# A two-block kernel whose first mixer begins with half of the features: modulation, tokens and weight rows come in two halves of the model width

## The chip, the cores and the metric

The kernel runs on one core of one Trainium2 chip. The metric is the device time of one execution, in microseconds (us). The engines are TensorE (PE; its weight loads are shown as PEld), VectorE (DVE), ScalarE (ACT), GpSimd (POOL) and SyncE (SP), whose queue issues nearly all DMA transfers.

## The reference: what is computed

Two transformer blocks, one after the other, on 256 tokens of width 1024 in float32. The change touches only the beginning of the first block:

```
mod = (jax.nn.silu(c) @ w_ada[l] + b_ada[l])[:, None, :]
shift_m, scale_m, gate_m, shift_f, scale_f, gate_f = jnp.split(mod, N_MOD, axis=-1)
h = rms_norm(x, g_mix[l]) * (1.0 + scale_m) + shift_m
x = x + gate_m * hybrid_mixer(h, w_in[l], b_forget[l], g_out_a[l], g_out_b[l], w_out[l])
...
proj = h @ w_in
(aq, ak, av, iq, ik, iw, bq, bk, bv, bf) = jnp.split(
    proj, list(np.cumsum(IN_SPLITS)[:-1]), axis=-1)
```

So the mixer's input `h` needs two of the six modulation vectors, `scale_m` (piece 1 of `w_ada`) and `shift_m` (piece 0), each a product of a vector of 1024 with a 1024 x 1024 part of `w_ada` (4 MB). Then come ten projections of `h` by column groups of `w_in` (1024 x 2896). After the mixer follow a mixture of 32 experts and the second block, which no line of the change touches.

## The kernel before, in words

All matrices are streamed from device memory once, in pieces of 1 MB (8 KB on each of 128 partitions), into a ring of 11 buffers (`raw`); an issue waits on SP until its buffer has been read for the last time. The SP queue issues in program order: four pieces of `w_ada` piece 0, `x`, four pieces of `w_ada` piece 1, and then the columns of `w_in` by projection (`iq`, `ik`, `bq`, `bk`, ...). Behind each load up to two small loads are let out of a list (`trickle`).

`ada(v)` makes modulation vector `v`. A piece of `w_ada` brings 2 of the 8 rows that each partition holds (row 8p+j lies on partition p), and 4 matmuls per piece (tile `p_ada`) sum them over all 8; the trace shows 8 rows for these 4. ScalarE copies the sums out (`part`), small matmuls turn them into columns (`p_col`), and VectorE adds the bias (`modcol`). The two square sums of `x`, `rstd`, and the normed tokens `xn` (shown as `prob`, whose buffer they use) follow from `x`; TensorE turns `xn` in 16 transposes (`p_tr`). `ac` is (1 + scale) times `g_mix`. `scaled` then makes the 8 slices (`j` = 0 to 7, 128 features each) of the turned and modulated input: `hTh` on ScalarE (rounded to fp32r), `full` on VectorE, and the rest `hTl` on VectorE or GpSimd.

Each projection is a generator of four steps of two slices `j` each. A step first cuts its weights in a high and a low part (`wih` on ScalarE, line 86; `wil` on VectorE, line 87) and then runs 24 matmuls (`p_w`: 2 slices, 4 column blocks, 3 products hi-hi, hi-lo, lo-hi). A projection's sums stay in two PSUM banks over its four steps. A string of letters sets the order of these steps: `i` (iq), `q` (bq), `k` (ik, iw and bf together), `b`, `v`, `a`, `n` are steps of projections, capitals are steps of the attention, of the indexer and of the rest; `F` begins with the matmul `p_dup`, which needs the result of `k`. The weights of a step are cut one step ahead of its products: where a letter is met, the products of the step before it are issued. Each engine's instructions run in the order in which they were issued or in which the framework's scheduler placed them; `held` fixes the order of those that it marks while `holding` is set.

In the kernel before, all 8 slices are modulated first, and then the string begins with `iiqikqqF`, so that the products ahead of `p_dup` are seven steps: i0, i1, i2, q0, i3, k, q1.

Of the kernel before, what the change touches and what calls it, by code (L numbers as in the profile page):

```python
# [7 lines left out]
FT = mybir.dt.float32  # L8
# [3 lines left out]
AF = mybir.ActivationFunctionType  # L12
OP = mybir.AluOpType
# [3 lines left out]
T = 256  # L17
D = 1024
# [14 lines left out]
def tile_block(ctx: ExitStack, tc: tile.TileContext, A, out):  # L33
# [12 lines left out]
    def bank(shape, name):  # L46
        return ps.tile(shape, FT, name=name, tag="bank")
# [5 lines left out]
    def load(name, shape, *src):  # L53
        n = 1
        for s in shape:
            n *= s
        t = raw.tile([128, RAW], FT, name=name, tag="raw")
        v = t[:, :n]
        if len(shape) == 2:
            v = v.rearrange("p (a b) -> p a b", a=shape[0])  # L60
        for i, s_ in enumerate(src):
            n = shape[0] // len(src)
            tc.keep_in_program_order(nc.sync.dma_start(v[:, n * i:n * i + n] if len(src) > 1 else v, s_))
        for _ in range(2):
            if trickle:
                dst, src_ = trickle.pop(0)
                tc.keep_in_program_order(nc.sync.dma_start(dst, src_))
        return v

    def load_cols(name, dname, width, c0, n, j0, nj):  # L70
        return load(name, (nj, n), dram(dname, j0 * width + c0,
                                        [[8 * width, 128], [width, nj], [1, n]]))

    holding = []

    def held(ins):
# [22 lines left out]
    def mm(o, lhsT, rhs, start, stop):  # L99
        held_pe(pe.matmul(o, lhsT, rhs, start=start, stop=stop, skip_group_check=True))  # L100
# [15 lines left out]
    c8 = const.tile([128, 8], FT, name="c8")  # L116
    act.dma_start(c8, dram("c", 0, [[8, 128], [1, 8]]))
    bcol = const.tile([128, 6, 8], FT, name="bcol")
    act.dma_start(bcol, dram("b_ada", 0, [[8, 128], [D, 6], [1, 8]]))
    gcol = const.tile([128, 2, 8], FT, name="gcol")  # L120
    act.dma_start(gcol[:, 0], dram("g_mix", 0, [[8, 128], [1, 8]]))
# [11 lines left out]
    def win_load(c0, n):  # L133
        return [load_cols(f"win{c0}_{k}", "w_in", WIN, c0, n, 4 * k, 4) for k in range(2)]

    xt = const.tile([128, 2, D], FT, name="xt")
    modrow = const.tile([128, 2, D], FT, name="modrow")
# [15 lines left out]
    aqk = raw2.tile([128, 8, T], FT, name="aqk", tag="raw2")  # L153
    aqT, akv, ikw, ikT = aqk[:, 0:4], aqk[:, 4:6], aqk[0:80, 6], aqk[:, 7]
    prob1 = raw2.tile([128, 8, T], FT, name="prob1", tag="raw2")
    for _ in range(4):
        ada_piece(0)
    tc.keep_in_program_order(nc.sync.dma_start(xt, dram("x", 0, [[D, 128], [128 * D, 2], [1, D]])))
    for _ in range(4):
        ada_piece(1)  # L160
    def small_load(dst, src):
        trickle.append((dst, src))

    w_bf = const.tile([128, 8, 8], FT, name="w_bf")
# [163 lines left out]
    def ada(v):  # L328
# [28 lines left out]
            dve.tensor_tensor(modcol[:, v - v // 3], p, bcol[:, v], op=OP.add)  # L357
        yield

    def gate_row():  # L360

        m = modrow[:, 1]
        for q in range(4):
            for jj in range(2):
                w = wada[5][q][:, jj]
                act.activation(w, w, AF.Copy, scale=cs[:, 2 * q + jj:2 * q + jj + 1])
                pool.tensor_tensor(m, m, w, op=OP.add)
            yield
# [26 lines left out]
        act.activation(junk, src, AF.Square, accum_out=s)  # L395
        return s

    def transpose_block(src, banks, t):
        for j in range(8):
            pe.transpose(banks[j // 2][:, j % 2, t * 128:t * 128 + 128], src[:, j::8], ident)  # L400

    def transposes(src, by_column=False):

        out_ = [bank([128, 2, T], "p_tr") for _ in range(4)]
        if by_column:
            for j in range(8):
                for t in range(2):
                    pe.transpose(out_[j // 2][:, j % 2, t * 128:t * 128 + 128], src[:, t, j::8], ident)
        else:
            for t in range(2):  # L410
                transpose_block(src[:, t], out_, t)
        return out_

    def scaled(banks, scale, bias, hi, lo, keep):

        for j in range(8):
            p = banks[j // 2][:, j % 2]
            sc = scale[:, j:j + 1]
            if bias is None:
                act.activation(hi[:, j], p, AF.Copy, scale=sc)  # L420
                dve.scalar_tensor_tensor(lo[:, j], p, sc, f32(hi[:, j]), op0=OP.mult, op1=OP.subtract)
            else:
                act.activation(hi[:, j], p, AF.Identity, bias=bias[:, j:j + 1], scale=sc)
                full = keep.tile([128, T], FT, name="full", tag="fin", bufs=3)
                dve.tensor_scalar(full, p, sc, bias[:, j:j + 1], op0=OP.mult, op1=OP.add)
                (dve if j % 2 else pool).tensor_tensor(lo[:, j], full, f32(hi[:, j]), op=OP.subtract)
# [8 lines left out]
    next(g1)  # L438
    xTb = [bank([128, 2, T], "p_tr") for _ in range(4)]
    for t in range(2):  # L440
        transpose_block(xn[:, t], xTb, t)
        next(g1)
    for _ in g1:
        pass
# [408 lines left out]
    def router_weights():  # L853
        dve.scalar_tensor_tensor(af, modcol[:, 3], 1.0, gcol[:, 1], op0=OP.add, op1=OP.mult)

        p = bank([36, 1], "p_rb")
        for j in range(8):
            mm(p, wr[:, j], bf_[:, j:j + 1], j == 0, j == 7)
        dve.tensor_tensor(wr, wr, af[:, :, None].to_broadcast([128, 8, 36]), op=OP.mult)
        dve.tensor_tensor(rb, rb, p, op=OP.add)  # L860
        rbr = const.tile([128, 36], FT, name="rbr")
        rbb = a1.tile([36, 128], FT, name="rbb", tag="fin", bufs=3)
        dve.tensor_copy(rbb, rb.to_broadcast([36, 128]))
        p = bank([128, 36], "p_rb")
        mm(p, rbb, ident[:36, :36], True, True)
        dve.tensor_copy(rbr, p)
        const_["rbr"] = rbr
        yield
# [8 lines left out]
            "Z": router_weights()}  # L877
    p_ = None
    for c in "iiqikqqFqXFXbbYYbbvY5TXXF22XY25XY5v5vYXYXv2BWBa2aaBYBnGB3BC33CCCC3BCanB3C!CR4D4D4D4E4DDDEoEHoEoDEoDEEESZpppp":
        if c == "!":  # L880
            flush()
        elif c == "p":
            if p_ is None:
                p_ = proj_out(1, *oa, rsa)
            main([next(p_)], 0)
        elif c.islower():
            main([next(work[c])], 0)
        else:
            next(work[c])
# [1060 lines left out]
```

## Time and profile before

| | before |
|---|---|
| runs (median, lowest to highest) | 741.2 us (740.72 to 742.93, 3 runs) |
| the profiled execution | 738.99 us, its span 737.2 us |
| mean granted TensorE clock | 0.966 |
| busy over the span: PE, DVE, ACT, POOL | 660.9, 402.3, 311.4, 88.9 us |
| moved by DMA | 196.94 MB, mean 267 GB/s |

The span runs from the first to the last instruction; the device time lies 1.79 us above it. A granted clock of 1.00 is TensorE's upper level (2.4 GHz), 0.50 its lower one (1.2 GHz). Matmul ends are modelled, so that a TensorE shown as busy isn't at its peak.

### The profile page before, as it was taken

To read this page: it belongs to the slowest core of one execution; us is meant where nothing else is said; L and a number is where in the kernel's file an instruction comes from. 1 tells how busy PE (TensorE), PEld (TensorE's weight loads), DVE (VectorE), ACT (ScalarE), POOL (GpSimd) and SP (SyncE) were. 2 spreads that over 40 slices of the span, in tenths; PEclk is the share of its full clock that TensorE was granted. 3 is DMA by queue.
4 is the path that set the end of the run, shared out by engine and by line. 5 is a ranking of instruction groups with operands and counts; after the bars stand their busy time and mean duration, and the time that the engine had idled before them with its cause. 6 is when DMAs were issued, how large, how long until landed. Compare 5 with 4: busy or idle time off the path is not lost. (4 is left out here: it accounts for less than half of the span.)

```text
span 737.2 us, 13263 instructions
## 1 busy us (share of the span) xinstructions
PE 660.9 (90%) x5489; PEld 510.4 (69%) x5489; DVE 402.3 (55%) x737; ACT 311.4 (42%) x513; POOL 88.9 (12%) x87
## 2 busy tenths in 40 slices
PE   5799996999899775998876989999999999999996
PEld 1498774877765333444442489987899999898994
DVE  2367978575663230423312269959676555555555
ACT  1446556564741010201110177685455444444445
POOL 7010309910000000000000063010000000000001
PEclk9899998999989998999988999999999999999999
DMA  9999779995639899998999999653445555550001
GB/s 342 372 382 359 257 273 292 307 405 206 261 133 421 322 421 415 405 397 332 422 418 420 374 370 387 212 172 116 138 149 172 172 192 201 177 199 34 1 1 57
DMA packets 69203, 196.94 MB, mean 267 GB/s; under 512 B 7550, under 2 KB 33219, under 8 KB 57350
## 3 DMA queue, kind: packets, MB, share of 16 engines
q1 hardware_dynamic: 67558, 195.30, 70.5%
q8 instruction: 53, 0.87, 0.5%
q10 hardware_dynamic: 1216, 0.30, 0.2%
q0 software_dynamic: 352, 0.28, 0.1%
q14 instruction: 24, 0.20, 0.1%
HBM read 194.81 MB, written 1.05 MB: 266 GB/s over the span
## 5 line engine op out<-in xcount | busy, mean ns | idle before, releaser
L100 PE MATMUL p_gu<-Xl,wguh 128*128 128x256 f32 x352 | 99.8, 284 | 0.0
L100 PE MATMUL p_gu<-Xh,wgul 128*128 128x256 f32 x352 | 99.3, 283 | 0.0
L100 PE MATMUL p_gu<-Xh,wguh 128*128 128x256 f32 x352 | 98.9, 283 | 0.1
L100 PEld LDWEIGHTS p_gu<-Xl,wguh 128*128 128x128 f32 x352 | 67.5, 192 | 0.5
L100 PEld LDWEIGHTS p_gu<-Xh,wguh 128*128 128x128 f32 x352 | 67.1, 192 | 0.7 <-ACT Xh L1379 0.4
L100 PEld LDWEIGHTS p_gu<-Xh,wgul 128*128 128x128 f32 x352 | 67.4, 192 | 0.3 <-DVE wgul L87 0.2
L100 PE MATMUL p_gu<-eg,xg 128*32 128x256 f32 x576 | 41.8, 416 | 15.3 <-PEq L1296 9.5
L87 DVE TENSOR_TENSOR wdnl<-wdn,wdnh 128x1024 fp32r<-128x1024 f32 x22 | 27.0, 1225 | 32.4 <-ACT wdnh L86 32.4
L100 PEld LDWEIGHTS p_gu<-eg,xg 128*32 128x32 f32 x576 | 19.7, 118 | 36.0 <-issue 24.4
L1149 DVE TENSOR_TENSOR sl<-sl,p_gu 128x256 f32<-128x256 f32 x9 | 3.8, 422 | 69.2 <-ACT sl L1148 69.2
L1148 ACT ACTIVATE sl<-p_gu 128x256 f32<-128x256 f32 x9 | 3.5, 384 | 87.9 <-PE p_gu L100 87.9
L100 PE MATMUL p_w<-hTh,wih 128*128 128x256 f32 x128 | 37.7, 297 | 2.5 <-ACT wih L86 2.5
L100 PE MATMUL p_dn<-ed,aT 128*32 128x512 f32 (+2 forms) x304 | 34.5, 573 | 5.2 <-ACT aT L1156 5.0
L86 ACT ACTIVATE wdnh<-wdn 128x1024 fp32r<-128x1024 f32 x22 | 23.3, 1058 | 36.5 <-PE p_gu L100 35.9
L87 DVE TENSOR_TENSOR wgul<-wup,wguh 128x1024 fp32r<-128x1024 f32 x22 | 27.0, 1226 | 21.3 <-ACT wguh L86 20.2
L1066 ACT ACTIVATE xg<-p_xg,modcol,af 128x128 f32<-128x128 f32 x36 | 15.6, 462 | 53.2 <-DVE xg L1068 53.0
L87 DVE TENSOR_TENSOR wgul<-wgt,wguh 128x1024 fp32r<-128x1024 f32 x22 | 27.0, 1225 | 19.8 <-ACT wguh L86 19.8
L86 ACT ACTIVATE wguh<-wgt 128x1024 fp32r<-128x1024 f32 x22 | 23.3, 1061 | 33.7 <-PE p_gu L100 18.2
L100 PE MATMUL p_w<-Xh,w2h 128*128 128x256 f32 x128 | 37.0, 289 | 0.5 <-ACT w2h L86 0.4
L100 PE MATMUL p_w<-Xh,w2l 128*128 128x256 f32 x128 | 36.3, 285 | 1.1 <-DVE w2l L87 0.6
L100 PE MATMUL p_w<-hTl,wih 128*128 128x256 f32 x128 | 36.9, 289 | 0.0
L100 PE MATMUL p_gu<-eu,xg 128*32 128x256 f32 x576 | 35.2, 379 | 1.9 <-DMA eu<-in_w_up_dram 1.9
(625 smaller groups left out, 1645.0 us busy)
## 6 DMA issues: line engine op xcount, KB each, us to landing
eg<-in_w_gate_dram SPq DMA_DIRECT2D x32, 1024.0 KB
eu<-in_w_up_dram SPq DMA_DIRECT2D x32, 1024.0 KB
ed<-in_w_down_dram SPq DMA_DIRECT2D x28, 1024.0 KB
wada<-in_w_ada_dram SPq DMA_DIRECT2D x24, 1024.0 KB
w<-in_w_in_dram SPq DMA_DIRECT2D x11, 1024.0 KB
wgt<-in_w_gate_up_dram SPq DMA_DIRECT2D x11, 1024.0 KB
wup<-in_w_gate_up_dram SPq DMA_DIRECT2D x11, 1024.0 KB
wdn<-in_w_down_dram SPq DMA_DIRECT2D x11, 1024.0 KB
```

What stands on the lines that cost most here:

```text
L86: held(act.activation(hi, src, AF.Copy))
L87: held(eng.tensor_tensor(lo, src, f32(hi), op=OP.subtract))
L100: held_pe(pe.matmul(o, lhsT, rhs, start=start, stop=stop, skip_group_check=True))
L1066: act.activation(xg[:, j], b[:, jj], AF.Identity, bias=bf_[:, j:j + 1], scale=af[:, j:j + 1])
L1148: act.activation(st.s[:st.n], st.b[:st.n, 0:256], AF.Silu)
L1149: dve.tensor_tensor(st.s[:st.n], st.s[:st.n], st.b[:st.n, 256:512], op=OP.mult)
```

## The change

Feature rows are dealt out anew for the first mixer: slices 0 to 3 now hold features 0 to 511 (four to a partition), slices 4 to 7 features 512 to 1023. `ada_cols(v, h)` makes one half (512 columns) of one modulation vector from two loads of 1 MB. `turn_half(h)` transposes one half of the tokens, and `modulated(h)` joins the two. The first half is made ahead of all products, the second is a letter of its own, `1`, in the string. The first halves of `w_in` for `iq` and `bq` are loaded ahead of the second halves of `w_ada`, and the string begins with `iqq1iikqF`, so that the products ahead of `p_dup` are i0, i1, q0, then q1, then i2, i3, k: the same seven steps.

```diff
+    def load_cols(name, c0, n, k=None):
+        src = [dram("w_in", 512 * WIN * h + c0, [[4 * WIN, 128], [WIN, 4], [1, n]]) for h in range(2)]
+        return load(name, (8, n), *src) if k is None else load(name, (4, n), src[k])
...
-    act.dma_start(bcol, dram("b_ada", 0, [[8, 128], [D, 6], [1, 8]]))
+    act.dma_start(bcol[:, 3:5], dram("b_ada", 3 * D, [[8, 128], [D, 2], [1, 8]]))
+    for v in range(2):
+        act.dma_start(bcol[:, v].rearrange("p (h j) -> p h j", h=2),
+                      dram("b_ada", v * D, [[4, 128], [512, 2], [1, 4]]))
...
+    def ada_half(v, h):
+        wada[v, h] = [load(f"wada{v}_{h}_{q}", (4, 512), dram("w_ada", 4 * q * 6 * D + v * D + 512 * h,
+                                                              [[8 * 6 * D, 128], [6 * D, 4], [1, 512]]))
+                      for q in range(2)]
...
-    for _ in range(4):
-        ada_piece(0)
+    ada_half(1, 0)
     tc.keep_in_program_order(nc.sync.dma_start(xt, dram("x", 0, [[D, 128], [128 * D, 2], [1, D]])))
-    for _ in range(4):
-        ada_piece(1)
+    ada_half(0, 0)
...
-    w_iq = win_load(768, 512)
-    w_ik = load_cols("wik", "w_in", WIN, 1280, 72, 0, 8)
+    w_iq = [load_cols("win768_0", 768, 512, 0)]
...
-    w_bq, w_bk, w_bv, w_aq = [], [], [], []
+    w_bq, w_bk, w_bv, w_aq = [load_cols("win1352_0", 1352, 512, 0)], [], [], []
+    ada_half(1, 1)
+    ada_half(0, 1)
+    w_iq.append(load_cols("win768_1", 768, 512, 1))
+    w_ik = load_cols("wik", 1280, 72)
...
+    def ada_cols(v, h):
+        p = bank([128, 512], "p_ada")
+        for q in range(2):
+            for r in range(4):
+                mm(p[32 * r:32 * r + 32], csr[:, 4 * q + r, :], wada[v, h][q][:, r], q == 0, q == 1)
+        yield
+        part = a1.tile([128, 512], FT, name="part", tag="fin", bufs=3)
+        held(act.activation(part.rearrange("p (j n) -> p j n", j=4), p.rearrange("p (n j) -> p j n", j=4), AF.Copy))
+        p = bank([128, 4], "p_col")
+        for j in range(4):
+            mm(p[:, j:j + 1], part[:, 128 * j:128 * j + 128], sel4, j == 0, True)
+        dve.tensor_tensor(modcol[:, v, 4 * h:4 * h + 4], p, bcol[:, v, 4 * h:4 * h + 4], op=OP.add)
+        yield
...
+    def turn_half(h):
+        xTb.extend(bank([128, 2, T], "p_tr") for _ in range(2))
+        for t in range(2):
+            for j in range(4):
+                pe.transpose(xTb[2 * h + j // 2][:, j % 2, t * 128:t * 128 + 128],
+                             xn[:, t, 512 * h + j:512 * h + 512:4], ident)
+
+    def modulated(h):
+        for v in (1, 0):
+            g = ada_cols(v, h)
+            next(g)
+            if v:
+                turn_half(h)
+            next(g)
+            if v:
+                hs = slice(4 * h, 4 * h + 4)
+                dve.scalar_tensor_tensor(ac[:, hs], modcol[:, 1, hs], 1.0, gcol[:, 0, hs], op0=OP.add, op1=OP.mult)
+        if h:
+            scaled(xTb, ac, modcol[:, 0], hTh, hTl, range(4, 8))
+        yield
...
     c0, m0 = next(st)
+    holding += [True]
+    next(modulated(0))
+    scaled(xTb, ac, modcol[:, 0], hTh, hTl, range(2))
     r0_ = c0()
-    scaled(xTb, ac, modcol[:, 0], hTh, hTl, a1)
+    scaled(xTb, ac, modcol[:, 0], hTh, hTl, range(2, 4))
+    del holding[:]
...
-    for c in "iiqikqqFqXFXbbYYbbvY5TXXF22XY25XY5v5vYXYXv2BWBa2aaBYBnGB3BC33CCCC3BCanB3C!CR4D4D4D4E4DDDEoEHoEoDEoDEEESZpppp":
+    for c in "iqq1iikqFqXFXbbYYbbvY5TXXF22XY25XY5v5vYXYXv2BWBa2aaBYBnGB3BC33CCCC3BCanB3C!CR4D4D4D4E4DDDEoEHoEoDEoDEEESZpppp":
```

TensorE's order at the program's begin, first of the kernel before, up to its first product `p_w` (`wada_0` to `wada_3` are the four loads of a piece, first of `w_ada` piece 0, then of piece 1):

```order
L100 MATMUL p_ada<-wada_0_95,csr 32x512 x4
L100 MATMUL p_ada<-wada_1_97,csr 32x512 x4
L100 MATMUL p_ada<-wada_2_99,csr 32x512 x4
L100 MATMUL p_ada<-wada_3_101,csr 32x512 x4
L100 MATMUL p_col<-selh,part 64x1 x16
L100 MATMUL p_ada<-wada_0_104,csr 32x512 x4
L400 MATMUL p_tr<-ident,prob_94 128x128 x8
L100 MATMUL p_ada<-wada_1_106,csr 32x512 x4
L400 MATMUL p_tr<-ident,prob_94 128x128 x8
L100 MATMUL p_ada<-wada_2_108,csr 32x512 x4
L100 MATMUL p_ada<-wada_3_110,csr 32x512 x4
L100 MATMUL p_col<-selh,part 64x1 x16
```

The same place now (`wada_0_0` and `wada_0_1` are the two loads of half 0, first of scale, then of shift):

```order
L102 MATMUL p_ada<-wada_0_0_97,csr 32x512 x4
L102 MATMUL p_ada<-wada_0_1_99,csr 32x512 x4
L462 MATMUL p_tr<-ident,prob_96 128x128 x8
L102 MATMUL p_col<-sel_215,part 128x1 x4
L102 MATMUL p_ada<-wada_0_0_102,csr 32x512 x4
L102 MATMUL p_ada<-wada_0_1_104,csr 32x512 x4
L102 MATMUL p_col<-sel_215,part 128x1 x4
L102 MATMUL p_w<-hTh,wih 128x256
```

Half of the modulation's products, half of the transposes and most of the `p_col` rows have left the place ahead of the first `p_w`.

The second halves of scale now stand on TensorE behind 72 products (i0, i1, q0), ahead of q1; the first load of shift's second half follows seven rows into q1:

```order
L102 MATMUL p_w<-hTh,wil 128x256
L102 MATMUL p_ada<-wada_1_0_121,csr 32x512 x4
L102 MATMUL p_ada<-wada_1_1_125,csr 32x512 x4
L462 MATMUL p_tr<-ident,prob_96 128x128 x8
L102 MATMUL p_col<-sel_215,part 128x1 x4
L102 MATMUL p_w<-hTh,wih 128x256
```

and its last load closes q1, directly ahead of the first product of i2:

```order
L102 MATMUL p_w<-hTh,wil 128x256
L102 MATMUL p_ada<-wada_1_1_133,csr 32x512 x4
L102 MATMUL p_col<-sel_215,part 128x1 x4
L102 MATMUL p_w<-hTh,wih 128x256
L102 MATMUL p_w<-hTl,wih 128x256
```

In the kernel before, only products stood between the first `p_w` and `p_dup`. Behind `p_dup` TensorE's order is that of before, but for one group of four `p_ada` rows (of gate, piece 2), which comes some 18 rows later, and a few score rows.

ScalarE around the second half, as it stands now (`win_1_137` holds the weights of i2 and i3, `win_0_117` those of q0 and q1):

```order
L88 ACTIVATE wih<-win_0_117 128x1024
L443 ACTIVATE hTh<-p_tr,modcol,ac 128x256
L88 ACTIVATE wih<-win_0_117 128x1024
L380 ACTIVATE part<-p_ada 128x512 x2
L443 ACTIVATE hTh<-p_tr,modcol,ac 128x256 x3
L88 ACTIVATE wih<-win_1_137 128x1024
L443 ACTIVATE hTh<-p_tr,modcol,ac 128x256
L88 ACTIVATE wih<-win_1_137 128x1024
```

The cut of i2's weights stands behind the second copy of sums (`part`) and three slices `hTh`; in the kernel before, the first cut stood behind two slices, and the later ones between slices.

## Rows read from the trace of the kernel before

**Rows 1.** Windows: busy us (x instructions) of PE, PEld, DVE, ACT, POOL; clock; DMA; GB/s.

```profile
33.30:55.90 22.60, 22.56 (x168) 22.27 (x169) 16.11 (x21) 12.05 (x18) 3.34 (x8) 0.88 1.05 378
55.90:96.70 40.80, 39.80 (x300) 32.64 (x299) 35.76 (x120) 22.69 (x32) 5.67 (x2) 1.00 0.85 314
...
131.00:200.00 69.00, 66.94 (x516) 54.82 (x517) 42.99 (x96) 41.95 (x87) 19.41 (x12) 0.98 0.82 308
200.00:222.00 22.00, 18.75 (x220) 12.56 (x222) 14.30 (x35) 10.13 (x16) 0.00 (x0) 0.84 0.34 127
222.00:400.00 178.00, 144.05 (x1645) 74.49 (x1645) 51.38 (x105) 19.59 (x53) 1.03 (x2) 0.95 0.97 397
...
423.00:737.20 314.20, 304.75 (x2117) 278.44 (x2115) 203.33 (x292) 172.01 (x238) 25.25 (x28) 1.00 0.47 162
```

**Rows 2.** Timeline, first 34 us, all engines: start, us, engine line op, out<-in, count [idle before].

```profile
6.36 1.94 PE L100 MATMUL p_ada<-wada,csr 128*32 128x512 f32 x8 [6.36 <-DMA wada<-in_w_ada_dram]
...
11.73 1.93 PE L100 MATMUL p_ada<-wada,csr 128*32 128x512 f32 x8 [0.70 <-DMA wada<-in_w_ada_dram]
...
14.30 1.93 PE L100 MATMUL p_ada<-wada,csr 128*32 128x512 f32 x8 [0.64 <-DMA wada<-in_w_ada_dram]
...
16.84 1.06 ACT L395 ACTIVATE prob<-xt 128x1024 f32<-128x1024 f32 x1
...
16.95 1.87 PE L100 MATMUL p_col<-selh,part 128*64 128x1 f32 x32 [0.72 <-ACT part L351]
...
21.77 1.95 PE L400 MATMUL p_tr<-ident,prob 128*128 128x128 f32 x8 [0.41 <-DVE rsr L390]
...
25.34 1.17 PE L400 MATMUL p_tr<-ident,prob 128*128 128x128 f32 x8
...
27.95 1.06 PE L100 MATMUL p_ada<-wada,csr 128*32 128x512 f32 x8 [0.44 <-DMA wada<-in_w_ada_dram]
...
29.73 1.10 PE L100 MATMUL p_col<-selh,part 128*64 128x1 f32 x32 [0.72 <-ACT part L351]
...
31.07 0.17 DVE L446 SCALAR_TENSOR_TENSOR ac<-modcol,gcol 128x8 f32<-128x8 f32 x1
31.28 1.02 ACT L423 ACTIVATE hTh<-p_tr,modcol,ac 128x256 fp32r<-128x256 f32 x2 [1.60 <-DVE ac L446]
...
32.19 1.05 ACT L86 ACTIVATE wih<-win 128x1024 fp32r<-128x1024 f32 x1
...
33.14 1.48 ACT L423 ACTIVATE hTh<-p_tr,modcol,ac 128x256 fp32r<-128x256 f32 x3
...
33.30 0.58 PE L100 MATMUL p_w<-hTh,wih 128*128 128x256 f32 x1 [2.47 <-ACT wih L86]
```

**Rows 3.** Timeline of TensorE: 25th product, two products 16 apart, and `p_dup`.

```profile
38.78 0.29 PE L100 MATMUL p_w<-hTh,wil 128*128 128x256 f32 x1
38.90 0.28 PE L100 MATMUL p_w<-hTh,wih 128*128 128x256 f32 x1
...
40.79 0.28 PE L100 MATMUL p_w<-hTl,wih 128*128 128x256 f32 x1
...
55.92 0.60 PE L100 MATMUL p_dup<-aqk,dup 80*128 80x256 f32 x2
```

**Rows 4.** Windows around the first product.

```profile
29.00:31.00 2.00, 1.11 (x34) 1.01 (x32) 0.12 (x1) 0.60 (x1) 0.00 (x0) 1.00 1.14 293
31.00:33.30 2.30, 0.01 (x1) 0.01 (x1) 0.78 (x4) 2.02 (x4) 0.73 (x1) 0.71 1.14 346
33.30:38.60 5.30, 5.26 (x23) 4.97 (x24) 5.30 (x9) 3.90 (x7) 0.91 (x2) 0.50 1.06 365
```

**Rows 5.** Timeline: `wil` cuts of VectorE, and the ACT issue of the last small load.

```profile
1.78 0.56 ACTq L121 DMA_DIRECT2D gcol<-in_g_mix_dram  x1
...
4.11 0.86 DVE L324 COPY csr<-cs 128x256 f32<-128x256 f32 x1
...
33.27 1.23 DVE L87 TENSOR_TENSOR wil<-win,wih 128x1024 fp32r<-128x1024 f32 x1 [0.85 <-ACT wih L86]
...
35.66 1.75 DVE L87 TENSOR_TENSOR wil<-win,wih 128x1024 fp32r<-128x1024 f32 x1
```

**Rows 6.** Timeline of SP's queue: issues that wait for buffers.

```profile
52.76 1.21 SPq L63 DMA_DIRECT2D wkv<-in_w_in_dram  x1
55.50 26.35 SPq L63 DMA_DIRECT2D wada<-in_w_ada_dram  x4
...
82.46 28.56 SPq L63 DMA_DIRECT2D wada<-in_w_ada_dram  x8
```

**Rows 7.** Timeline, 113 to 128 us: VectorE and TensorE in the softmax of `C`.

```profile
113.58 1.29 DVE L732 TENSOR_REDUCE bmx<-p_sc 128x2 f32<-128x512 f32 x2 [2.12 <-PE p_sc L100]
...
127.13 1.94 PE L754 MATMUL p_pt<-ident,prob 128*128 128x128 f32 x8 [6.84 <-DVE brc L746]
```

More of the change, by code (lines that the diff above doesn't have):

```diff
@@ L68, in load @@
         return v
-    def load_cols(name, dname, width, c0, n, j0, nj):
-        return load(name, (nj, n), dram(dname, j0 * width + c0,
-                                        [[8 * width, 128], [width, nj], [1, n]]))
+    def load_cols(name, c0, n, k=None):
+        src = [dram("w_in", 512 * WIN * h + c0, [[4 * WIN, 128], [WIN, 4], [1, n]]) for h in range(2)]
+        return load(name, (8, n), *src) if k is None else load(name, (4, n), src[k])
     holding = []
@@ L118, in tile_block @@
     bcol = const.tile([128, 6, 8], FT, name="bcol")
-    act.dma_start(bcol, dram("b_ada", 0, [[8, 128], [D, 6], [1, 8]]))
+    act.dma_start(bcol[:, 3:5], dram("b_ada", 3 * D, [[8, 128], [D, 2], [1, 8]]))
+    for v in range(2):
+        act.dma_start(bcol[:, v].rearrange("p (h j) -> p h j", h=2),
+                      dram("b_ada", v * D, [[4, 128], [512, 2], [1, 4]]))
     gcol = const.tile([128, 2, 8], FT, name="gcol")
-    act.dma_start(gcol[:, 0], dram("g_mix", 0, [[8, 128], [1, 8]]))
+    act.dma_start(gcol[:, 0].rearrange("p (h j) -> p h j", h=2), dram("g_mix", 0, [[4, 128], [512, 2], [1, 4]]))
     wada = {}
@@ L131, in tile_block @@
     WIN = 2896
-    def win_load(c0, n):
-        return [load_cols(f"win{c0}_{k}", "w_in", WIN, c0, n, 4 * k, 4) for k in range(2)]
+    def ada_half(v, h):
+        wada[v, h] = [load(f"wada{v}_{h}_{q}", (4, 512), dram("w_ada", 4 * q * 6 * D + v * D + 512 * h,
+                                                              [[8 * 6 * D, 128], [6 * D, 4], [1, 512]]))
+                      for q in range(2)]
     xt = const.tile([128, 2, D], FT, name="xt")
@@ L164, in tile_block @@
     w_bf = const.tile([128, 8, 8], FT, name="w_bf")
-    small_load(w_bf, dram("w_in", 2888, [[8 * WIN, 128], [WIN, 8], [1, 8]]))
+    for h in range(2):
+        small_load(w_bf[:, 4 * h:4 * h + 4], dram("w_in", 512 * WIN * h + 2888, [[4 * WIN, 128], [WIN, 4], [1, 8]]))
     small_load(gcol[:, 1], dram("g_ffn", 0, [[8, 128], [1, 8]]))
@@ L206, in tile_block @@
         wada[v] = []
-    for name in 'bq bq bk 2 2 bk bv bv 3 5 aq kv 2 2 3 3 aq 3 5 5 5 4 4 4 4'.split():
+    for name in 'bq bk 2 2 bk bv bv 3 5 aq kv 2 2 3 3 aq 3 5 5 5 4 4 4 4'.split():
         if name == "kv":
-            w_kv = load_cols("wkv", "w_in", WIN, 512, 256, 0, 8)
+            w_kv = load_cols("wkv", 512, 256)
         elif name in COLS:
@@ L212, in tile_block @@
             k = len(later[name])
-            later[name].append(load_cols(f"win{c0}_{k}", "w_in", WIN, c0, n, 4 * k, 4))
+            later[name].append(load_cols(f"win{c0}_{k}", c0, n, k))
         else:
@@ L280, in tile_block @@
         dve.memset(selh[32 * q:32 * q + 1, q % 2], 1.0)
+    sel4 = a1.tile([128, 1], FT, name="sel4")
+    dve.tensor_tensor(sel4, selh[:, 0, 0:1], selh[:, 1, 0:1], op=OP.add)
     dup = a1.tile([80, 128], FT, name="dup")
@@ L396, in sumsq @@
         return s
-    def transpose_block(src, banks, t):
-        for j in range(8):
-            pe.transpose(banks[j // 2][:, j % 2, t * 128:t * 128 + 128], src[:, j::8], ident)
     def transposes(src, by_column=False):
@@ L410, in transposes, with scaled @@
             for t in range(2):
-                transpose_block(src[:, t], out_, t)
-        return out_
-    def scaled(banks, scale, bias, hi, lo, keep):
-        for j in range(8):
+                for j in range(8):
+                    pe.transpose(out_[j // 2][:, j % 2, t * 128:t * 128 + 128], src[:, t, j::8], ident)
+        return out_
+    def scaled(banks, scale, bias, hi, lo, js):
+        for j in js:
             p = banks[j // 2][:, j % 2]
             sc = scale[:, j:j + 1]
[L419 to L426, printed above, removed]
+            held(act.activation(hi[:, j], p, AF.Identity, bias=bias[:, j:j + 1], scale=sc))
+            full = a1.tile([128, T], FT, name="full", tag="fin", bufs=3)
+            held(dve.tensor_scalar(full, p, sc, bias[:, j:j + 1], op0=OP.mult, op1=OP.add))
+            held((dve if j % 2 else pool).tensor_tensor(lo[:, j], full, f32(hi[:, j]), op=OP.subtract))
     xn = prob1.rearrange("p (t a) b -> p t (a b)", t=2)
-    g0, g1 = ada(0), ada(1)
-    for _ in g0:
-        pass
     for t in range(2):
@@ L437, in tile_block @@
         dve.tensor_scalar(xn[:, t], xt[:, t], r, None, op0=OP.mult)
[L438 to L444, printed above, removed]
-    ac = small.tile([128, 8], FT, name="ac")
-    dve.scalar_tensor_tensor(ac, modcol[:, 1], 1.0, gcol[:, 0], op0=OP.add, op1=OP.mult)
+    xTb = []
+    ac = small.tile([128, 8], FT, name="ac")
+    def turn_half(h):
[17 more added lines that the diff above has]
+        yield
     rsa = const.tile([128, 2], FT, name="rsa")
@@ L876, in tile_block @@
             "G": gate_out(0), "H": gate_out(1), "T": turn_rows(), "W": loads1(), "R": rstd_b(), "S": rstd_a(),
-            "Z": router_weights()}
+            "Z": router_weights(), "1": modulated(1)}
     p_ = None
-    for c in "iiqikqqFqXFXbbYYbbvY5TXXF22XY25XY5v5vYXYXv2BWBa2aaBYBnGB3BC33CCCC3BCanB3C!CR4D4D4D4E4DDDEoEHoEoDEoDEEESZpppp":
+    for c in "iqq1iikqFqXFXbbYYbbvY5TXXF22XY25XY5v5vYXYXv2BWBa2aaBYBnGB3BC33CCCC3BCanB3C!CR4D4D4D4E4DDDEoEHoEoDEoDEEESZpppp":
         if c == "!":
```

## The prediction

> **What bounds the kernel now.** I read the busy time by stage first, then the timeline of the first 34 us, then TensorE's rows up to `p_dup`, then the queue of SP.
>
> Up to the first product at 33.30 the loads set the pace. TensorE's groups of `p_ada` each wait for a load of 1 MB; the first starts at 6.36, the fourth at 14.30, so a load takes (14.30 - 6.36) / 3 = 2.65 us [rows 2]. Nine loads (`w_ada` twice 4 MB, `x`) must land, and the last group starts at 27.95. Behind it comes a chain on which TensorE only waits: from its end at 27.95 + 1.06 = 29.01 to 33.30 are 4.29 us, made of the copy of sums, `p_col` (1.10), the bias, `ac` (31.07, with 0.21 to the next step), two slices `hTh` and one cut `wih` [rows 2].
>
> From 33.30 the reader is to see the opposite: TensorE is busy 22.56 of 22.60 us up to 55.9 [rows 1]. Seven steps of 24 products stand there. At the upper clock 16 products take 40.79 - 38.90 = 1.89, so a step takes 24 x 1.89 / 16 = 2.83 us; the first one takes 38.78 - 33.30 = 5.48 [rows 3], since it runs at the lower clock, granted clock 0.50 [rows 4]. 33.30 + 5.48 + 6 x 2.83 = 55.76, and `p_dup` stands at 55.92 [rows 3]. So nothing but TensorE's own work lies between, and I take the start of `p_dup` as the mark: TensorE's order behind it is that of before.
>
> What happens behind the mark passes a delay on, nearly one to one. TensorE is busy 39.80 of the next 40.80 us and 66.94 of 69 from 131 to 200. From 200 to 222 DMA is at 0.34: the ring is full and the expert loads wait for the mixer to end. From 222 to 400 it is at 0.97, so this stretch lasts as long as its loads and begins when buffers come free. From 423 TensorE is busy 304.75 of 314.2 us [rows 1].
>
> **The change, part by part.**
>
> *The first product comes earlier.* `x` is now the third load instead of the fifth, so it lands where the third group starts now, 11.73. From the first square sum to the first transpose are 21.77 - 16.84 = 4.93 us [rows 2], which gives 16.66. On TensorE then follow, all at the lower clock's rows: eight transposes 1.95 (to 18.61), one `p_col` of 8 trace rows, 1.87 x 8 / 32 = 0.47 (to 19.08), and two groups `p_ada` of 1.94 (to 22.96; their loads, the fourth and fifth, landed by 14.30 and 16.95) [rows 2]. The chain behind is the old one without `ac`, which is made ahead, and with the shorter `p_col`: 4.29 - 1.10 - 0.21 + 0.47 = 3.45. First product at 26.41: 6.89 us earlier.
>
> *The second half's work now lies between products.* In the old place it was hidden behind the loads; that cover is gone, because TensorE has no free time up to the mark. Four groups `p_ada` at 1.06 are 4.24, eight transposes 1.17, the `p_col` of scale 1.10 x 8 / 32 = 0.28 [rows 2]: 5.69 us. Its loads aren't late: the tenth 1 MB lands near 6.36 + 9 x 2.65 = 30, and TensorE comes to it after 40.
>
> *A second break.* The last group `p_ada` stands directly ahead of `p_col` and the first product of i2, and TensorE keeps to its order. So the chain of the beginning is walked a second time with nothing beside it: 4.29 - 1.10 - 0.21 + 0.28 = 3.26, and ScalarE now has three slices ahead of the cut of i2 instead of two, 1.48 - 1.02 = 0.46 more [rows 2]. Together 3.72 us. Late next is the low cut `wil` of i2, behind three `full` on VectorE; this cut took 1.23 or, beside GpSimd's work, 1.75 [rows 5], so 0 to 0.5 us more. I take 0.
>
> *The clock.* The break at 29.01 to 33.30, with 1.10 us of `p_col` in it, was followed by the lower level: 0.71 in the break, 0.50 in the first step, which cost 5.48 - 2.83 = 2.65 us [rows 3, 4]. The first break of the changed kernel is much like it, so i0 stays as it was. The second one (3.72 with 0.28 of work) is as empty, and nothing in these rows makes it milder: i2 is likely to pay the 2.65 again. Bounds: 0, if the upper level holds; 5.3, if i3 is low as well. The Trainium skill, TensorE: Matmul & The Clock Gate, section "HAM oscillation — how this bites in real kernels", says that a TensorE that waits between bursts falls back to half rate, and that each burst then starts slow; by it the second break costs its restart too, and the sum is +5.2 and not +2.5. The trace agrees in the one case of this stage, 0.50 behind the break at 29.01.
>
> *Parts that cost nothing.* The two more small issues on ScalarE's queue (0.56 each [rows 5]) push `csr` from 4.97 to about 6.1, still ahead of the first load at 6.36; without that cover they would cost up to 1.1. Rows of 2 KB instead of 4 KB in the half loads: the stretch whose loads are 2 KB rows of `w_in` and 4 KB rows ran at 378 GB/s [rows 1], 2.77 us per MB, so `x` may land 0.1 x 3 = 0.4 later; bounds 0 and 0.4, and I take 0, since no row separates the two. On SP the order of loads behind `wik` is that of before, but for `bq`. The first wait for buffers there begins at 55.50 [rows 6], and the buffers that the later `p_ada` groups hold come free before 47.
>
> *Sum at the mark.* -6.89 + 5.69 + 3.72 + 2.65 = +5.17: i2's first product near 49.8, `p_dup` near 61.1. The profiled execution took 738.99, which gives 744.2. The median of the three runs shown is 741.2, 2.2 us above that execution, and a measurement is compared with such runs: 746.4 us. About 0.3% (2.2 us) is what a measurement of this kernel can tell from no change.
>
> **The rivals.**
>
> *Only one of the two breaks is followed by the lower clock.* For it: a single break is thin evidence, and whether TensorE is at the upper level when the first break begins isn't sure; today it gets there by 25.34, where transposes take 1.17 instead of 1.95 [rows 2]. Against: the one comparable break did bring the clock down. +2.52, 743.7. Chance 0.22.
>
> *TensorE reaches the upper level in the run of work from 16.66 on and keeps it over both breaks* (the other side). Then neither i0 nor i2 pays (-2.65 each from the forecast), and the work ahead of the first product shrinks: `p_ada` 3.88 to 2.12, `p_col` 0.47 to 0.28, and transposes by 0.5 (their second half waits for the second token tile), together 2.45. 5.17 - 5.3 - 2.45 = -2.58: 738.6. It decides as soon as more than 5.17 us of these 7.75 are saved. For it: from 16.66 to 22.96 TensorE would work without a gap, where today it pauses between loads. Against: it must hold through 3 us of waiting twice, and it didn't once [rows 4]. Chance 0.09.
>
> *The delay is absorbed behind the mark.* TensorE waits 6.84 us for VectorE before `p_pt` of the softmax `C` [rows 7]; work that is late only on TensorE would vanish there. Against: VectorE's own chain there starts 2.12 us late, on TensorE's `p_sc` [rows 7], so it moves too. If half is swallowed: about +2, 743. Chance 0.12.
>
> *The change doesn't do what it says: the first product is hardly earlier*, since the loads in half rows, or the small ones between them, are slower. A delay of 0.5 us for each of the first five loads is +2.5: 748.9. Against: `p_ada` at 6.36 and the even 2.65 [rows 2]. Chance 0.07.
>
> **How the numbers follow.** The forecast, +5.17, has 0.50, and its own range is 744 to 749. The range over all: down to 740, which leaves out the clock's best case (0.09), up to 749 (i3 low too, 741.2 + 7.8). Faster by over 0.3%: the clock's best case and a little for what no row shows, 0.12. Within 0.3%: half of the first rival, which lies right at the edge, and most of the absorption, 0.25. Slower: 0.63.
>
> **What would show it.** Right: first `p_w` at 26 to 27; four groups `p_ada` of about 1.06 and eight transposes between products; a TensorE break of 3 to 4 us right ahead of i2, ended by `wih`; granted clock 0.50 for some us behind it; `p_dup` near 61; all later stages shifted alike. Wrong: `p_dup` before 56, a clock of 1.00 behind both breaks, or a stage behind the mark that is shorter than before by more than 2 us.

## The result

The changed kernel takes 753.11 us (median of 4 runs, 752.12 to 754.28), the kernel before 741.96 us beside it (4 runs, 740.72 to 742.93): ratio 1.0155, 95% interval 1.0132 to 1.0177. It is slower by 11.15 us, where +5.2 was forecast. The direction was right; the time lies above the whole range (740 to 749). The profiled execution took 753.72 us (span 752.0, mean granted clock 0.950).

TensorE's timeline after, from its first group to the first product (columns as in [rows 2], its counterpart):

```profile
7.22 1.93 PE L102 MATMUL p_ada<-wada,csr 128*32 128x512 f32 x8 [7.22 <-DVE csr L336]
...
17.02 1.95 PE L462 MATMUL p_tr<-ident,prob 128*128 128x128 f32 x8 [5.96 <-DVE rsr L417]
18.77 1.70 PE L102 MATMUL p_col<-sel,part 128*128 128x1 f32 x8
20.40 3.64 PE L102 MATMUL p_ada<-wada,csr 128*32 128x512 f32 x16
24.75 1.05 PE L102 MATMUL p_col<-sel,part 128*128 128x1 f32 x8 [0.72 <-ACT part L380]
28.78 0.58 PE L102 MATMUL p_w<-hTh,wih 128*128 128x256 f32 x1 [2.98 <-ACT wih L88]
```

The first product starts at 28.78, so 4.52 us earlier than 33.30 [rows 2], not 6.89. Each `p_col` has a quarter of the rows of before's (8 for 32), yet takes 1.70 and 1.05 us, nearly as much as those of before (1.87 and 1.10).

The same view from the second half to `p_dup`, the counterpart of [rows 3]; rows left out are products:

```profile
34.48 0.32 PE L102 MATMUL p_w<-hTh,wih 128*128 128x256 f32 x1
...
40.30 1.92 PE L102 MATMUL p_ada<-wada,csr 128*32 128x512 f32 x16
42.16 1.23 PE L462 MATMUL p_tr<-ident,prob 128*128 128x128 f32 x8
43.22 0.95 PE L102 MATMUL p_col<-sel,part 128*128 128x1 f32 x8
...
45.05 1.06 PE L102 MATMUL p_ada<-wada,csr 128*32 128x512 f32 x8
48.23 1.06 PE L102 MATMUL p_ada<-wada,csr 128*32 128x512 f32 x8
...
50.08 1.05 PE L102 MATMUL p_col<-sel,part 128*128 128x1 f32 x8 [0.78 <-ACT part L380]
54.11 0.58 PE L102 MATMUL p_w<-hTh,wih 128*128 128x256 f32 x1 [2.98 <-ACT wih L88]
...
54.91 0.41 PE L102 MATMUL p_w<-hTl,wih 128*128 128x256 f32 x1
56.20 0.58 PE L102 MATMUL p_w<-hTh,wil 128*128 128x256 f32 x1 [0.87 <-DVE wil L89]
...
61.70 0.36 PE L102 MATMUL p_w<-hTh,wil 128*128 128x256 f32 x1
61.90 0.28 PE L102 MATMUL p_w<-hTh,wih 128*128 128x256 f32 x1
...
64.02 0.28 PE L102 MATMUL p_ik<-hTh,ikh 128*80 128x256 f32 x1
...
67.47 0.70 PE L102 MATMUL p_dup<-aqk,dup 80*128 80x256 f32 x2
```

Read it as the sum was made. Work of the second half stands at 40.30 to 44.03 and at 45.05 and 48.23. Behind the last `p_ada` (48.23 + 1.06 = 49.29) TensorE has only a `p_col` until 54.11. But for a wait for `wil` (0.87 of idle time), the products that follow stand 0.21 us apart up to 61.70 and 0.12 apart from 61.90 on. `p_dup` starts at 67.47, 11.55 us later than before.

ScalarE from the last copy of sums on, to see what fills the second break (then VectorE's first low cut):

```profile
49.43 0.60 ACT L380 ACTIVATE part<-p_ada 128x512 f32<-128x512 f32 x1 [6.54 <-PE p_ada L102]
51.37 1.02 ACT L443 ACTIVATE hTh<-p_tr,modcol,ac 128x256 fp32r<-128x256 f32 x2 [1.34 <-DVE modcol L384]
52.54 0.56 ACT L443 ACTIVATE hTh<-p_tr,modcol,ac 128x256 fp32r<-128x256 f32 x1 [0.16 <-DVE full L445]
53.01 1.04 ACT L88 ACTIVATE wih<-win 128x1024 fp32r<-128x1024 f32 x1
...
54.39 1.76 DVE L89 TENSOR_TENSOR wil<-win,wih 128x1024 fp32r<-128x1024 f32 x1
```

Windows after (columns as in [rows 1]): the second break, i2 and what follows it, then two that answer to [rows 1], the stretch behind `p_dup` and the last part:

```profile
50.00:54.10 4.10, 1.05 (x8) 0.97 (x8) 1.66 (x5) 2.55 (x5) 0.72 (x1) 0.70 1.05 389
54.10:66.00 11.90, 11.02 (x65) 10.73 (x66) 6.28 (x10) 5.43 (x8) 3.92 (x6) 0.67 1.04 392
67.40:108.30 40.90, 39.91 (x296) 32.05 (x295) 36.14 (x121) 22.59 (x33) 5.66 (x2) 1.00 0.59 213
438.00:752.00 314.00, 305.29 (x2120) 278.76 (x2118) 203.43 (x293) 171.89 (x238) 25.08 (x28) 0.99 0.47 163
```

The clock is 0.70 in the break and 0.67 over the 11.9 us behind it (0.71 and 0.50 in [rows 4], whose last window ends with i0); stages behind the mark are as full as they were, only later. `p_dot`, which needs `p_dup`, starts at 71.1 (59.9 before), the softmax `C` reaches `p_pt` at 138.0 (127.1, [rows 7]), the expert products begin at 221.9 (207.1), the span ends 14.8 later. Of these, 11.2 are there at `p_dot`. The other 3.6 us are of this pair of executions: the profiled run of before lies 3.0 us below its median, that of after 0.6 above its own.

### The profile page after: what moved, and what is told of

Read it like the earlier page. It is cut to its first block, busy times and chain, and to the rows that moved or that the text cites. A ratio compares the mean times of both kernels' runs of the same rounds, so it can differ in the third digit from the quotient of the medians.

```text
span 752.0 us, 13211 instructions
## 1 busy us (share of the span) xinstructions
PE 669.7 (89%) x5457; PEld 521.4 (69%) x5457; DVE 402.6 (54%) x741; ACT 312.9 (42%) x515; POOL 91.5 (12%) x87
## 3 DMA queue, kind: packets, MB, share of 16 engines
HBM read 194.81 MB, written 1.05 MB: 260 GB/s over the span
## 5 line engine op out<-in xcount | busy, mean ns | idle before, releaser
L102 PE MATMUL p_w<-hTh,wih 128*128 128x256 f32 x128 | 39.5, 308 | 6.0 <-ACT wih L88 6.0
L102 PE MATMUL p_w<-hTh,wil 128*128 128x256 f32 x128 | 38.2, 302 | 0.9 <-DVE wil L89 0.9
L102 PE MATMUL p_w<-hTl,wih 128*128 128x256 f32 x128 | 38.5, 301 | 0.0
L102 PE MATMUL p_xg<-Pq,xn 128*128 128x128 bf16 x384 | 27.3, 238 | 10.7 <-ACTq L1217 7.0
```

## The experiments

All ratios are against the kernel before, run beside each on the same chip (its median was 740.9 to 742.5). `p_dot` is the mark here, since orders differ in what stands just ahead of `p_dup`. "Rest" is the span from `p_dot` to the last instruction.

| kernel | median us | ratio, 95% interval | first product | `p_dot` | rest |
|---|---|---|---|---|---|
| before | 741.96 | 1 | 33.30 | 59.9 | 677.3 |
| after | 753.11 | 1.0155 (1.0132 to 1.0177) | 28.78 | 71.1 | 680.9 |
| e1_letter_earlier | 744.96 | 1.0045 (1.0022 to 1.0067) | 29.47 | 65.5 | 677.6 |
| e2_warm_second | 761.93 | 1.0270 (1.0225 to 1.0314) | 29.70 | 69.4 | 691.1 |
| e3_halves_all_ahead | 754.18 | 1.0175 (1.0128 to 1.0222) | 41.27 | 66.9 | 685.4 |
| e3b_free | 750.90 | 1.0145 (1.0120 to 1.0170) | 37.63 | 66.7 | 682.2 |
| e4_unheld | 751.51 | 1.0149 (1.0122 to 1.0176) | 26.78 | 68.8 | 680.4 |
| e5_before_warm | 742.39 | 1.0008 (0.9986 to 1.0031) | 34.83 | 59.0 | 679.7 |
| e6_col64 | 756.98 | 1.0226 (1.0200 to 1.0253) | 28.15 | 68.5 | 684.8 |
| e7_all_three | 741.72 | 1.0013 (0.9991 to 1.0035) | 26.17 | 60.7 | 679.0 |
| e8_x_first | 738.26 | 0.9960 (0.9932 to 0.9988) | 22.55 | 57.5 | 678.4 |
| e9_before_x_first | 740.03 | 0.9994 (0.9961 to 1.0027) | 33.61 | 60.4 | 676.9 |

**e1: the letter one step earlier,** so that 48 products more cover the end of the second half's chain.

```diff
-    for c in "iqq1iikqF...":
+    for c in "iq1qiikqF...":
```

Expected: 

> The letter 1 stands one place earlier (iq1qiikqF), so that the 48 products of q0 and q1 stand behind the second half's last column product and ahead of i2. Theory (the delay is made on TensorE ahead of p_dup: second half's work 5.9 us, second break 4.8, lower clock behind it 4.2): the break ahead of i2 shrinks to under 1 us, the clock stays at 1.00 there, p_dup moves from 67.5 to about 60.3 and the time from 753 to about 746. Rival (the half loads, the order of loads or the buffers hold the stage): p_dup stays within 1 us of 67.5 and the time at 752 to 754, since no load has moved.

TensorE at the place of the second half (transposes and a group left out), then the window around the first products of i2:

```profile
38.51 1.06 PE L102 MATMUL p_ada<-wada,csr 128*32 128x512 f32 x8
...
42.45 1.05 PE L102 MATMUL p_col<-sel,part 128*128 128x1 f32 x8 [0.72 <-ACT part L380]
43.43 1.92 PE L102 MATMUL p_ada<-wada,csr 128*32 128x512 f32 x16
46.13 1.05 PE L102 MATMUL p_col<-sel,part 128*128 128x1 f32 x8 [0.78 <-ACT part L380]
```

```profile
50.00:56.00 6.00, 6.00 (x54) 6.00 (x53) 5.00 (x8) 2.78 (x6) 3.93 (x6) 1.00 1.05 385
```

The work of the second half is there in full, and now waits 0.72 and 0.78 for its copies, so it takes 47.04 - 38.51 = 8.53 us. But there is no break ahead of i2, no lower clock behind it, and `p_dot` is 5.6 us earlier than after the change. Net of that longer work and of a first product 0.69 us later, the edit gives back half of the loss at the mark, and it came in the time: 744.96, 3.95 above the kernel before instead of 11.15. `p_dup` moved to 62.7, not to the expected 60.3.

**e2: filler products in the second break,** 12 matmuls (24 rows) of `p_warm` ahead of the slices. **e5: the same in the one break of the kernel before,** 10 matmuls. The fillers add work that computes nothing.

```diff
         if h:
+            warm(12)
             scaled(xTb, ac, modcol[:, 0], hTh, hTl, range(4, 8))
```

Expected of e2: 

> 12 matmuls that nobody reads stand in the second break, between the last column product and i2. Theory (the lower clock behind the break costs 3.4 to 4.2 us): the break stays at 4.8 us, the granted clock stays at 1.00, i2 and i3 together take about 6.5 us instead of 9.9, p_dup at about 64, time about 749.7. Rival (i2 is held by the cuts on ScalarE and VectorE, not by the clock): i2 and i3 keep 9 us or more, time 752 to 754.

Expected of e5: 

> The kernel before with 10 matmuls that nobody reads in its one break, between the last column product and the first product. Theory (the first step pays 2.65 us for the lower clock): the granted clock stays at 1.00, the first step takes about 3 us instead of 5.5, p_dup at about 53.4, time about 739.3 against 742. Rival (the first step is held by slices and cuts, which come at about the pace of the slow products): the first step keeps 4.5 us or more, time within 1 us of before.

TensorE of e2 at the second break, and far behind it; then its windows at both places:

```profile
51.86 2.92 PE L110 MATMUL p_warm<-ones,ident 128*128 128x128 f32 x24
54.98 0.39 PE L102 MATMUL p_w<-hTh,wih 128*128 128x256 f32 x1 [0.19 <-ACT wih L88]
57.06 0.39 PE L102 MATMUL p_w<-hTh,wil 128*128 128x256 f32 x1 [1.35 <-DVE wil L89]
...
62.33 0.28 PE L102 MATMUL p_ik<-hTh,ikh 128*80 128x256 f32 x1
...
111.43 3.78 PE L102 MATMUL p_row<-part,selh 128*128 128x512 f32 x4 [3.68 <-DVE part L356]
```

```profile
55.00:66.00 11.00, 9.65 (x77) 9.25 (x78) 7.25 (x10) 5.59 (x9) 3.63 (x6) 1.00 1.04 392
111.40:118.00 6.60, 6.57 (x21) 4.51 (x22) 3.04 (x6) 5.33 (x20) 0.00 (x0) 0.54 1.00 390
```

The break is as long as it was (4.80), the clock stays at 1.00 behind it, and i2 and i3 take 62.33 - 54.98 = 7.35 us for 64.02 - 54.11 = 9.91: the clock was a real part of the loss. `p_dot` is only 1.7 us earlier than after the change (69.4 for 71.1), since the first product came 0.9 later. The wait for `wil` is still there, 1.35, so it is a term of its own. The total was missed by 12 us: at 111.43 TensorE had waited 3.68 us for VectorE's `part` (2.01 after the change), and the lower clock fell on what follows. In e5 the fillers took the place of the break, and the lower clock came all the same, but it fell on the fillers (the last two rows are the first and the 25th product):

```profile
30.94 4.13 PE L108 MATMUL p_warm<-ones,ident 128*128 128x128 f32 x20
34.83 0.36 PE L100 MATMUL p_w<-hTh,wih 128*128 128x256 f32 x1
...
37.75 0.28 PE L100 MATMUL p_w<-hTh,wih 128*128 128x256 f32 x1
```

```profile
31.00:33.30 2.30, 2.30 (x15) 2.30 (x14) 0.88 (x3) 1.83 (x3) 0.61 (x1) 0.59 1.13 335
```

The products behind the fillers stand 0.12 us apart, and the first step takes 37.75 - 34.83 = 2.92 us, as the theory had it (about 3). But the slow fillers kept TensorE until the first product, 1.53 later than before (34.83 for 33.30). Together `p_dot` came 0.9 earlier, nothing that the time shows. So fillers held the clock once; the other time it fell all the same, and they took the slow rows in place of products.

**e3: both halves ahead of all products,** with before's order of loads and steps; **e3b: the same without the fixed order** (`holding`).

```diff
     ada_half(0, 0)
+    ada_half(1, 1)
+    ada_half(0, 1)
...
-    for c in "iqq1iikqF...":
+    for c in "iiqikqqF...":
```

Expected of e3: 

> The halved form alone: both halves of scale and shift are loaded and made ahead of all products, and loads and steps of the projections have the old order (iiqikqqF). Theory (the halved form costs little, its place among the products costs): first product at about 35.5 (six slices stand ahead of the first cut, 2 us more than before), p_dup at about 58, time about 744. Rival (the halved form itself, its 2 KB rows and its column products with 128 columns of weights, makes most of the delay): p_dup above 63, time above 748.

Expected of e3b: 

> Both halves made ahead of all products, in the old order of loads and steps, without the fixed order of slices: the halved form alone. Theory (the form costs little by itself; the loss comes from its place among the products): first product near 35.5, p_dup near 58, median near 743.5. Rival (halved loads, groups and p_col cost several us wherever they stand): first product above 38, median above 747.

The theory of both missed. First ScalarE of e3 at its slices, then TensorE of e3b:

```profile
35.91 0.56 ACT L442 ACTIVATE hTh<-p_tr,modcol,ac 128x256 fp32r<-128x256 f32 x1 [0.16 <-DVE full L444]
37.54 1.02 ACT L442 ACTIVATE hTh<-p_tr,modcol,ac 128x256 fp32r<-128x256 f32 x2 [1.07 <-DVE full L444]
39.70 0.56 ACT L442 ACTIVATE hTh<-p_tr,modcol,ac 128x256 fp32r<-128x256 f32 x1 [1.15 <-DVE full L444]
40.17 1.05 ACT L88 ACTIVATE wih<-win 128x1024 fp32r<-128x1024 f32 x1
```

```profile
33.61 1.05 PE L102 MATMUL p_col<-sel,part 128*128 128x1 f32 x8 [0.72 <-ACT part L379]
37.63 0.50 PE L102 MATMUL p_w<-hTh,wih 128*128 128x256 f32 x2 [2.97 <-ACT wih L88]
```

In e3 six slices stand ahead of the cut, and ScalarE waits for `full` three times there (0.16, 1.07 and 1.15). Without the fixed order (e3b) only three do, and one such wait (0.16); later slices still wait for `full` (1.63, 1.40), so the turns that the two engines take aren't the fixed order's work alone. In e3b the first product is still 4.33 us later than before: four chains of copy, `p_col` and bias stand one behind the other, where before had two, and from 20 us on no group of `p_ada` waits for its load. So the rival comes nearer (first product 37.63 where it said above 38, median 750.90 where it said above 747): the halved form, with its `p_col` over 128 weight columns, costs several us in this place too.

**e4: the changed kernel without the fixed order.**

```diff
-    holding += [True]
...
-    del holding[:]
```

Expected: 

> The changed kernel without the fixed order around the first half: ScalarE now cuts both weights of i0 ahead of the slices, and VectorE and ScalarE need not take turns slice by slice. Theory (the first product comes late because the marked slices take turns with `full`, 0.61 us of waiting, and `wih` stands behind four of them): first product near 27.2 instead of 28.78, p_dup near 66, median near 751.5. Rival (the order is nothing; the chain is bound by p_col and modcol alone): first product within 0.4 of 28.78, median within 1 us of 753.1.

The first product moved to 26.78 (28.78), `p_dup` to 65.1 and `p_dot` to 68.8, so the order was worth 2.0 us at the first product and 2.3 at `p_dot`: ScalarE cuts `wih` at 21.10, ahead of the slices, and the first product waits for its first slice alone. The intervals of the ratios overlap with that of the change, so the total (751.51, as expected) neither shows nor denies it.

**e6: `p_col` over 64 weight columns,** twice as many matmuls.

```diff
-            mm(p[:, j:j + 1], part[:, 128 * j:128 * j + 128], sel4, j == 0, True)
+            for o in (0, 64):
+                mm(p[o:o + 64, j:j + 1], part[:, 128 * j + o:128 * j + o + 64], sel4, j == 0, True)
```

Expected: 

> The changed kernel with each p_col in two matmuls over 64 weight columns instead of one over 128. Theory (a row of 128 columns costs about 0.13 us at the upper level, where the kernel before paid 0.034 for 64): each p_col takes 0.3 to 0.55 instead of 1.05 and 0.5 to 1.0 instead of 1.70, so some 2 us less up to p_dup (three p_col lie on the path), p_dup near 65.4, median near 751. Rival (what the rows show is the fill of the pipeline, whatever the columns): p_col stays above 0.9, median within 1 us of 753.1.

A `p_col` of the first half (at the lower level), the last one of the second half (at the upper one), and a wait far behind:

```profile
18.84 1.02 PE L102 MATMUL p_col<-sel,part 128*64 128x1 f32 x16
...
48.20 0.63 PE L102 MATMUL p_col<-sel,part 128*64 128x1 f32 x16 [0.78 <-ACT part L380]
...
110.46 3.46 PE L102 MATMUL p_row<-part,selh 128*128 128x512 f32 x4 [3.70 <-DVE part L356]
```

The price falls nearly as far as the theory had it, 1.02 for 1.70 and 0.63 for 1.05, and `p_dot` comes 2.6 us earlier. The 64-column form, like that of before, also writes the two halves of its columns in turn, which no run takes apart from the columns. Against that as the reason stands `p_rb` of the changed kernel: its rows have 36 weight columns, are all written to the same place, and stand 0.04 us apart at a granted clock of 1.00 (TensorE's timeline after the change):

```profile
184.91 0.72 PE L102 MATMUL p_rb<-modcol,wr 128*36 128x1 f32 x16
```

The total went the other way, to 756.98. The place is that of e2: VectorE is busy 28.95 of the 29.7 us up to 109.7, its `part` starts at 109.71 (109.57 after the change, with `p_dot` 2.6 later), and `p_row` waits 3.70 and then runs slow. From `p_dot` to that `part` VectorE is busy 38.25 of 41.21 us in e6 and 35.82 of 38.47 after the change, with nearly the same rows (122 and 123). They stand in another order, and one cut `wbvl`, during GpSimd's rows of `modrow`, takes 3.28 (2.11 at most after the change); which of the two is the reason isn't shown. An earlier `p_dot` buys nothing while VectorE, as full as TensorE there, takes that much longer.

**e7: the three edits of e1, e4 and e6 together.**

Expected: 

> The changed kernel with three edits at once: the letter of the second half one step earlier, no fixed order around the first half, p_col over 64 columns. Theory (the three losses add up): first product near 26.5, no break ahead of i2, p_dot near 62 (59.9 before, 71.1 after the change), median near 743.3, so within 0.5% of the kernel before but not faster. Rival (with the breaks gone the early first product is a gain): p_dot below 59.5, median below 740.

741.72: no difference from before that can be measured, as the theory said. TensorE of e7 in i0 and at both ends of the second half's work:

```profile
27.97 0.58 PE L102 MATMUL p_w<-hTl,wih 128*128 128x256 f32 x1 [1.01 <-POOL hTl L447]
...
35.46 1.92 PE L102 MATMUL p_ada<-wada,csr 128*32 128x512 f32 x16
...
42.24 0.38 PE L102 MATMUL p_w<-hTh,wih 128*128 128x256 f32 x1
```

The first product is 7.13 earlier than before, and the second half's work takes 42.24 - 35.46 = 6.78 between products; i0 and i1 take 9.29 for 5.60 + 2.83 = 8.43, since a product waits 1.01 for `hTl`. -7.13 + 6.78 + 0.86 = +0.51, and `p_dot` stands at +0.8. That is what the form is worth without its three losses.

**e8: e7 with `x` as the first load; e9: the kernel before with `x` as the first load.**

```diff
+    tc.keep_in_program_order(nc.sync.dma_start(xt, dram("x", 0, [[D, 128], [128 * D, 2], [1, D]])))
     ada_half(1, 0)
-    tc.keep_in_program_order(nc.sync.dma_start(xt, dram("x", 0, [[D, 128], [128 * D, 2], [1, D]])))
```

Expected of e8: 

> The kernel with the three edits (letter earlier, no fixed order, p_col over 64 columns), and `x` as the first load instead of the third. In the run with the three edits the transposes start at 17.10 since `x` lands near 12.1, and the 3.64 us of the products of shift stand behind them. Theory (with `x` first the transposes are done before the fourth and fifth load land, and the first product hangs on the fifth load alone): first product near 23.3 instead of 26.17, p_dot near 57.8 (59.9 before), median near 739, so 0.2 to 0.5% faster than the kernel before. Rival (the weights of i0, which land near 19.6 and are cut behind two slices, or the second half's loads take the place of the wait): first product above 25 or p_dot above 60, median 741 or more.

Expected of e9: 

> The kernel before with `x` as the first load instead of the fifth, nothing else. Theory (its first product hangs on the ninth load and the chain behind it, so the tokens are not what it waits for): first product within 0.5 of 33.30, median within 2 us of 741. Rival (earlier transposes free TensorE ahead of the last groups): first product below 32, median below 739.

TensorE of e8 at the last group and the first product:

```profile
17.87 1.06 PE L102 MATMUL p_ada<-wada,csr 128*32 128x512 f32 x8 [1.13 <-DMA wada<-in_w_ada_dram]
...
22.55 0.58 PE L102 MATMUL p_w<-hTh,wih 128*128 128x256 f32 x1 [2.27 <-ACT wih L88]
```

Now the last `p_ada` waits for its load (1.13), and the first product is at 22.55. The time, 738.26, is the only one whose whole interval lies below the kernel before: 0.4%, 0.9932 to 0.9988. In e9 the same move changed nothing, since there the ninth load sets the first product (33.61). So here the halves paid only where they, and not the tokens, were what the first product waited for.

## Why the prediction was right in direction and half in size

| term | predicted | measured |
|---|---|---|
| *the first product comes earlier* | -6.89 | -4.52 |
| i0 stays as it was | 0 | 34.48 - 28.78 - 5.60 = +0.10 |
| *the second half's work* between products | +5.69 | 3.73 + 1.08 + 1.06 = +5.87 |
| *a second break* | +3.72 | 54.11 - 49.29 = +4.82 |
| *the clock* and `wil`, over i2 and i3 | +2.65 | 64.02 - 54.11 - 2 x 2.83 = +4.25 |
| rest | 0 | +1.0, of it 0.63 for four products of q2 that stand ahead of `p_dup` |
| sum at `p_dup` | +5.17 | +11.55 |

The 5.60 is the first step of before up to its 25th product at 38.90 [rows 3]; the row at 38.78, from which the prediction took 5.48, is the 24th. With it the lower clock cost 2.77 us there, not 2.65.

**The mechanism was right,** and sizes were off. Products came earlier, the second half's work stood uncovered between them, a second break ahead of i2 ended with `wih`, the lower clock followed it, and the delay was passed on behind the mark. e1 takes the break away, and the wait for `wil` and the lower clock go with it; e2 takes the clock alone. Of the rivals, neither the break without the lower clock nor the absorbed delay came; loads that hold up the first product were at most 0.36 of it.

**The price of `p_col`** is the step that failed most. It was put at a quarter of before's, because a quarter as many rows stand there: 1.50 us in its four places, which measured 4.75 (1.70, 1.05, 0.95 and 1.05). These 3.25 us are half of the 6.38 by which the sum was too low, and the range allowed for a slow i3, not for them. But each row now has 128 weight columns where it had 64: 1.70 / 8 = 0.21 us a row, for 1.87 / 32 = 0.058 [rows 2]. e6 has 0.064 and 0.039 with 64. The Trainium skill, TensorE: Matmul & The Clock Gate, section "LDWEIGHTS (loading the stationary operand)", says that a weight load's time goes by its number of columns; the trace agrees in the direction, and the rows of `p_col` show more than in proportion, 0.131 for 0.039 at the upper level.

**The first product** was 2.37 us later than said. Of the 2.37, 1.23 and 0.58 are the two `p_col`, 0.36 is `x` (landed by 12.09 for 11.73; 0.4 was the bound that was set aside), 0.61 the second slice's wait for `full`, under the fixed order; transposes and groups took 0.4 less than priced. e4, without that order, gives 2.0 back.

**The second break** was 1.10 longer: `p_col` 1.05 for 0.28, and most of the rest is the third slice, which waited 0.16 for `full` (no order is fixed there).

**The clock** was priced nearly right: 29 products stood 0.21 instead of 0.12 apart, 29 x (0.213 - 0.118) = 2.76. What was missed is the wait for the low cut `wil`, taken as 0 between bounds of 0 and 0.5. It was 56.20 - 54.91 - 0.21 = 1.08: `wil` came behind a low slice on VectorE and took 1.76. The Trainium skill's rule, in the section "HAM oscillation — how this bites in real kernels" of the same page, that each burst behind a long wait starts slow, held here: 0.67 behind the break. The waits of 0.72 and 0.78 us in e1 had no lower clock behind them (1.00).

**Parts that cost nothing.** `csr` was later than said (TensorE's first group waited for it until 7.22, not 6.1), but that group isn't on the path, since the transposes wait for `x`. The first wait for buffers on SP did no harm that the rows show.

**Passed on one to one** held for the change and for e1, e4, e7, e8 and e9 (rest 676.9 to 680.9 us). It did not hold for e2, e3, e3b and e6, which lost 5 to 14 us behind the mark. In e2 and e6 one place is known, VectorE ahead of `p_row` and the slow rows behind it: up to the softmax `C` it holds 6.5 of the 13.8 us in e2 and 5.1 of the 7.5 in e6. Why VectorE took longer there was not tried, and the rest was not traced. Of e3's 8.1 us, 5.4 arise between the last row of `p_wo` (197.3) and the first expert product (222.0); their cause is open.

## What to carry to other kernels

Before work is moved from behind loads into a run of products, add up what has to be uncovered in it: here 5.9 us of work against some 7 that an earlier start could win, so that even without the break the form came out about even (e7). Put such a late piece so that its last link, from sums through columns, slices and cuts, still has products beside it: one letter in the order was worth 5.6 us. And price a small matmul by its weight columns, not by the number of its rows.

## What the runs showed of the hardware

A trace row of a matmul of one column (two rows each) over 128 weight columns of float32 took 0.21 us at the lower level and 0.13 at the upper one; over 64 columns, with halves in turn, 0.064 and 0.039. The record of the granted clock shows 1.00 until its first event, although rows are those of the lower level: in e7 the stretch from 26.17 to 35.46 is given as 1.00, and its products stand 0.21 us apart up to 31.98. And 20 filler rows, with no pause between them, did not keep the clock from falling in e5 (0.59), while 24 did in e2; in e5 the products behind them stood at the upper level again.
